# First modulation vectors with the raw weights stationary, and four weight pieces loaded ahead of the vectors' second half

## The chip, the cores and the metric

The kernel runs on one core of one Trainium2 chip. The metric is the device time of one execution in microseconds (us), from the first to the last instruction of the program with what lies around it; lower is better. The time before is 2695.26 us, the median of three runs (2690.73, 2696.66, 2695.26).

The core has five engines that run side by side and wait for each other through semaphores: TensorE (PE) for matrix products, VectorE (DVE), ScalarE (ACT), GpSimd (POOL), and SyncE (SP), which in this kernel issues nearly all transfers (DMAs). A matmul consists of a weight load (PEld in the profile), which puts the stationary operand into the array, and of the matmul proper, which moves the other operand past it, column by column.

## The reference

One layer of a backbone: a modulated RMSNorm, a mixer with one shared input projection, a gated residual, a second modulated norm and an MLP. There are 17 tiles of 128 tokens: tile 0 is context, tiles 1 to 16 are latent tokens. Context and latent tokens have a conditioning vector each (c_ctx and c), so all modulation vectors exist twice. What the change touches is this part:

```python
def modulation(cond, w_mod_l, b_mod_l):
    m = jax.nn.silu(cond) @ w_mod_l + b_mod_l
    return jnp.split(m[:, None, :], N_MOD, axis=-1)
...
    sh1, sc1, ga1, sh2, sc2, ga2 = mod
    h = rmsnorm(x, norm_mix_l) * (1.0 + sc1) + sh1
    o, s_new = mixer(h, s0, n_chunks, w_in_l, conv_l, a_log_l, dt_bias_l, o_norm_l, ws_l, bs_l, w_out_l)
...
    proj = h @ w_in_l
```

The model width is 1024, so each of the six modulation vectors has 1024 elements and w_mod is 1024 x 6144. The first norm needs sh1 (columns 0 to 1023 of w_mod) and sc1 (columns 1024 to 2047). Everything is float32.

## The kernel before

**Number formats.** The large products run three times on operands split into a high and a low part (mm3, lines 217 to 219: high x high, low x high or high x low). split_w (line 191 on ACT, line 192 on DVE) splits a weight piece of 128x512. The first modulation vectors are not split: mod_columns multiplies plain float32, for which TensorE runs each matmul as two records, each with a weight load of its own.

**Buffers.** Pieces of 128x512 come from one pool, tag "w", 49 buffers; raw_w (line 182) loads one of 256 KB. The tag "x" has three buffers of 128x1024. pm1() gives one of two PSUM banks, pt() one of three, pj() one of three.

**The start.** The conditioning vectors, through silu, stand in scond: for each of the 8 pieces k of the width, 128 rows by 2 columns (context, latent). mod_load(half, c0) loads eight pieces of w_mod, 512 columns of one vector: m0 is the first half of sh1, m1 that of sc1, m2 and m3 the second halves. mod_columns then needs the result as columns: feature on the partition, one column per conditioning vector. It does so in three steps. Eight matmuls with scond[:, k, :] stationary (128x2) move the raw piece (512 columns) and add up to a row pair of 2x512 in PSUM (line 321). ACT copies the pair to SBUF (line 323). Four transposes (line 326) turn its 128-column pieces into columns in a second PSUM bank. DVE adds the bias (line 329), and for sc1 adds 1 and multiplies by the norm's weight (line 333), into b1 and a1.

**The halo and the first tokens.** xh holds the ten token rows at the borders of the token blocks, in a buffer of the tag "x". norm_rows (ACT line 304, POOL line 176, DVE line 306) scales rows to unit size; eight transposes (line 373) bring xh into columns, hal. Then the three tiles of block 0 are loaded into buffers of the same tag "x" (line 378) and normalised; the third of them takes the buffer that xh had, and so waits for xh's transposes.

**Block 0.** first_half(half) modulates four pieces of hal (lines 393 to 397). column(k) of prep_block makes the modulated, transposed input of piece k: three transposes (line 468), ACT's scale and shift with a1 and b1 (line 470), and DVE's split into kH and kL (lines 473 and 474), which SP stores (lines 486 and 487). Step k of feature_tile (project) multiplies one 128x128 part of the weight piece W1[gi][k] with kH and kL: three matmuls of 388 columns. Three feature tiles run together in block 0, nine matmuls for each k. ab_block (lines 595 and 596) is a small projection of the same input. So steps k 0 to 3 need the first halves of sh1 and sc1 and the first four pieces of W1[1], steps k 4 to 7 the second halves and the other four.

**Order.** The text of the program doesn't set the order on an engine. A scheduler, which runs a simulated timeline while the program is built, takes what is ready, with the order of the text as a priority. In the text the loads of m2 and m3 come first, then those of four pieces of W1[1] (wr), then mod_columns(m1), steps k 0 to 3 of block 0, and mod_columns(m2) and (m3).

Of the kernel before, what the change touches and what calls it, by code (L numbers as in the profile page):

```python
# [8 lines left out]
F32 = mybir.dt.float32  # L9
# [8 lines left out]
P = 128  # L18
D = 1024
KT = D // P  # L20
# [41 lines left out]
def hybrid_step(  # L62
# [7 lines left out]
    V, A, G, T = nc.vector, nc.scalar, nc.gpsimd, nc.tensor  # L70
# [41 lines left out]
    ident = cp.tile([P, P], F32, name="ident")  # L112
# [49 lines left out]
    scond = cp.tile([P, KT, 2], F32, name="scond")  # L162
# [6 lines left out]
    def pm1():  # L169
        return pmp.tile([P, 512], F32, tag="pm", name="pm", bufs=2)  # L170
# [9 lines left out]
    def raw_w(src, pool=None, tag="w"):  # L180
        t = (pool or wp).tile([P, 512], F32, tag=tag, name="raw")
        load(out=t, in_=src)
        return t
# [83 lines left out]
    with ExitStack() as ph:  # L267
        p1 = ph.enter_context(tc.tile_pool(name="p1", bufs=2, reuse_waits="tile"))
        pf = ph.enter_context(tc.tile_pool(name="p1f", bufs=2, reuse_waits="tile"))
# [43 lines left out]
        def mod_load(half, c0):  # L313
            return [raw_w(w_mod[0, k * P : (k + 1) * P, c0 + half * 512 : c0 + half * 512 + 512])
                    for k in range(KT)]

        def mod_columns(raws, half, dst, bias, scaled):

            pm = pm1()
            for k in range(KT):  # L320
                T.matmul(pm[0:2, :], scond[:, k, :], raws[k], start=k == 0, stop=k == KT - 1)  # L321
            row = p1.tile([2, 512], F32, tag="mrow", name="mrow", bufs=1)
            A.copy(row, pm[0:2, :])
            pc = pm1()
            for i in range(4):
                T.transpose(pc[:, 2 * i : 2 * i + 2], row[:, i * P : (i + 1) * P], ident[0:2, 0:2])
            ks = slice(half * 4, half * 4 + 4)
            d = dst[:, :, ks]
            V.tensor_tensor(out=d, in0=pc[:, 0:8].rearrange("p (k c) -> p c k", c=2),
                            in1=bias[:, ks].unsqueeze(1).to_broadcast([P, 2, 4]), op=ALU.add)  # L330
            if scaled:
                for cd in range(2):
                    V.scalar_tensor_tensor(out=dst[:, cd, ks], in0=dst[:, cd, ks], scalar=1.0,
                                           in1=vec[:, 16 + half * 4 : 20 + half * 4], op0=ALU.add, op1=ALU.mult)
# [23 lines left out]
        convw = vec[:, 32:68].rearrange("p (w a) -> p w a", w=3)  # L358
        m1 = mod_load(0, D)
        mod_columns(m0, 0, b1, vec[:, 0:8], False)  # L360


        xh = p1.tile([P, D], F32, tag="x", name="xh", bufs=3)[0:10, :]
        for m in range(5):
            r0 = 255 + 384 * m
            load(out=xh[2 * m : 2 * m + 2, :], in_=x_sample[0, r0 : r0 + 2, :])
# [9 lines left out]
        for t in BLOCKS[0]:  # L376
            x = p1.tile([P, D], F32, tag="x", name="x", bufs=3)
# [5 lines left out]
        def load_w1(gi, ks):  # L383
            return [w1_raw(gi, k) for k in ks]

        def w1_raw(gi, k):
            return raw_w(w_in[0, k * P : (k + 1) * P, gi * 512 : (gi + 1) * 512])
# [327 lines left out]
        blk, xs_, cols = prep_block(0)  # L715
        for st in xs_:
            st()
        m2 = mod_load(1, 0)
        m3 = mod_load(1, D)
        wr = load_w1(1, range(4))  # L720
        mod_columns(m1, 0, a1, vec[:, 8:16], True)
        W1[1] += [split_w(r) for r in wr]
        first_half(0)
# [3 lines left out]
        wr = load_w1(0, range(KT))  # L727
        us = [feature_tile(blk, 0, 1, h) for h in range(3)]
        for k in range(4):
            cols[k]()  # L730
            for u in us:
                u["main"][k]()
        mod_columns(m2, 1, b1, vec[:, 0:8], False)
        mod_columns(m3, 1, a1, vec[:, 8:16], True)
        W1[1] += [split_w(r) for r in wk]
# [1016 lines left out]
    raws, sops = {}, {}  # L1752
# [91 lines left out]
    for m, (n, i, u, q) in enumerate(todo):  # L1844
# [20 lines left out]
        if i in (1, 5, 6) and mm < 28:  # L1865
            while pending and mm >= pending[0][0] + 2:
                _, k, r = pending.pop(0)
# [60 lines left out]
```

## Time and profile before

| | |
|---|---|
| median of three runs | 2695.26 us (2690.73 to 2696.66) |
| the profiled execution | 2696.7 us |
| its span, from first to last instruction | 2695.0 us |
| mean granted clock of TensorE | 0.993 |
| busy: TensorE, its weight loads, DVE, ACT, POOL | 2628.5, 2192.3, 1866.8, 1245.5, 229.5 us |
| the 64 records of line 321 | 30.5 us |

How to read it. Views quoted are of one profiled execution; times are us from the start of its span unless marked ns. L321 is line 321 of the kernel. In a group, "out<-in" names tiles, then come partitions x elements and the count, busy time and mean ns of one, and the idle time of the engine just before with what ended it. In the timeline and in the chain of waits, the first number is the start, the second the duration. Matmuls are pipelined: a row of several overlapping matmuls gives the time from the start of the first to the end of the last, so the pace is that time less one duration, over the count less one. In a table of windows stand the length, then busy us and count of PE, PEld, DVE, ACT and POOL, the granted clock of TensorE (1.00 is full), the mean busy share of the 16 DMA engines, and GB/s.

### The profile page before, as it was taken

To read this page: it belongs to the slowest core of one execution; us is meant where nothing else is said; L and a number is where in the kernel's file an instruction comes from. 1 tells how busy PE (TensorE), PEld (TensorE's weight loads), DVE (VectorE), ACT (ScalarE), POOL (GpSimd) and SP (SyncE) were. 2 spreads that over 40 slices of the span, in tenths; PEclk is the share of its full clock that TensorE was granted. 3 is DMA by queue.
4 is the path that set the end of the run, shared out by engine and by line. 5 is a ranking of instruction groups with operands and counts; after the bars stand their busy time and mean duration, and the time that the engine had idled before them with its cause. 6 is when DMAs were issued, how large, how long until landed. Compare 5 with 4: busy or idle time off the path is not lost.

```text
span 2695.0 us, 45202 instructions
## 1 busy us (share of the span) xinstructions
PE 2628.5 (98%) x15698; PEld 2192.3 (81%) x15698; DVE 1866.8 (69%) x3909; ACT 1245.5 (46%) x3092; POOL 229.5 (9%) x448
## 2 busy tenths in 40 slices
PE   8999999999999899999999999999999999999998
PEld 5999997788887787778887788888888787888887
DVE  5867656877777878885688775665565547774874
ACT  4655555555555656763355543332342432342441
POOL 3111203111111111110000000000000000000000
PEclk9999999999999999999999999999999999999999
DMA  8867539555555657885877797433459979876772
GB/s 297 279 202 224 183 113 299 177 157 161 160 162 157 204 191 232 269 279 181 285 221 228 212 313 228 122 104 106 121 170 371 329 265 309 272 243 215 235 252 94
DMA packets 569388, 580.91 MB, mean 216 GB/s; under 512 B 35693, under 2 KB 401693, under 8 KB 565575
## 3 DMA queue, kind: packets, MB, share of 16 engines
q1 hardware_dynamic: 569158, 578.03, 67.2%
q8 instruction: 123, 2.02, 0.3%
q14 instruction: 107, 0.87, 0.1%
HBM read 398.14 MB, written 179.74 MB: 214 GB/s over the span
## 4 chain that ended last, share of the span: by engine, by line
PE 86%; DVE 6%; DMA 5%; issue 1%; ACT 1%; POOL 0%; SPq 0%; DVEq 0%; POOLq 0%; ACTq 0%
PE f L219 17%; PE f L217 17%; PE f L218 17%; PE pj L217 6%; PE pj L219 6%; PE pj L218 6%; PE pd L959 3%; PE pm L217 1%; PE pm L219 1%; PE pm L218 1%; PE pm L321 1%; PE pt L575 1%; PE pd L1136 1%; PE pd L1137 1%; DMA qT<-qT_d 1%
## 5 line engine op out<-in xcount | busy, mean ns | idle before, releaser
L217 PE MATMUL f<-hop,zH 128*128 128x512 f32 x960 | 376.5, 393 | 1.2 <-ACT zH L1444 1.2
L218 PE MATMUL f<-hop,zH 128*128 128x512 f32 x960 | 377.1, 393 | 0.0
L219 PE MATMUL f<-hop,zL 128*128 128x512 f32 x960 | 376.9, 393 | 0.0
L217 PE MATMUL f<-hop,wH 128*128 128x512 f32 x896 | 354.0, 397 | 0.0
L219 PE MATMUL f<-hop,wL 128*128 128x512 f32 x896 | 351.3, 392 | 0.0
L218 PE MATMUL f<-hop,wH 128*128 128x512 f32 x896 | 351.1, 392 | 0.0
L1444 ACT CAST zH<-zraw 128x512 fp32r<-128x512 f32 x240 | 146.6, 620 | 287.2 <-DVE zraw L1438 86.4
L217 PEld LDWEIGHTS f<-hop,zH 128*128 128x128 f32 x960 | 180.3, 188 | 43.7 <-ACT zH L1444 1.6
L219 PEld LDWEIGHTS f<-hop,zL 128*128 128x128 f32 x960 | 180.3, 188 | 41.9 <-issue 0.9
L218 PEld LDWEIGHTS f<-hop,zH 128*128 128x128 f32 x960 | 180.2, 188 | 41.8 <-issue 0.9
L1438 DVE TENSOR_TENSOR zL<-zraw,zH 128x512 fp32r<-128x512 f32 x240 | 162.9, 686 | 69.1 <-ACT zH L1444 57.7
L219 PEld LDWEIGHTS f<-hop,wL 128*128 128x128 f32 x896 | 168.5, 188 | 37.7
L218 PEld LDWEIGHTS f<-hop,wH 128*128 128x128 f32 x896 | 168.8, 188 | 35.2
L217 PEld LDWEIGHTS f<-hop,wH 128*128 128x128 f32 x896 | 168.8, 188 | 34.7
L217 PE MATMUL pj<-kH,wH 128*128 128x386 f32 (+2 forms) x568 | 190.5, 338 | 0.3 <-DVE kH L473 0.3
L219 PE MATMUL pj<-kH,wL 128*128 128x386 f32 (+2 forms) x568 | 190.3, 335 | 0.0
L218 PE MATMUL pj<-kL,wH 128*128 128x386 f32 (+2 forms) x568 | 189.5, 334 | 0.0
L176 POOL TENSOR_TENSOR r<-rsq,nhalf 128x1 f32<-128x1 f32 (+1 forms) x38 | 23.0, 606 | 1499.3 <-DVE rsq L175 1499.3
L1438 DVE TENSOR_TENSOR wL<-raw,wH 128x512 fp32r<-128x512 f32 x112 | 76.0, 687 | 76.0 <-ACT wH L1444 74.9
L523 DVE SCALAR_TENSOR_TENSOR cv<-pj,vec,cv 128x384 f32<-128x384 f32 (+2 forms) x164 | 87.1, 539 | 58.7 <-ACT cv L520 57.4
L217 PEld LDWEIGHTS pj<-kH,wH 128*128 128x128 f32 x568 | 107.2, 189 | 4.6 <-issue 4.2
L217 PE MATMUL pj<-wH,hH 128*128 128x512 f32 x248 | 109.8, 443 | 0.0
(398 smaller groups left out, 6088.3 us busy)
## 6 DMA issues: line engine op xcount, KB each, us to landing
zraw<-z_d SPq DMA_DIRECT2D x212, 256.0 KB
raw<-in_w_ff_dram SPq DMA_DIRECT2D x128, 256.0 KB
hop<-hop_d SPq DMA_DIRECT2D x28, 1024.0 KB
z_d<-c SPq DMA_DIRECT2D x96, 256.0 KB
zraw<-s_d SPq DMA_DIRECT2D x96, 256.0 KB
raw<-in_w_mod_dram SPq DMA_DIRECT2D x80, 256.0 KB
r<-in_w_ff_dram SPq DMA_DIRECT2D x80, 256.0 KB
s_d<-s SPq DMA_DIRECT2D x64, 256.0 KB
```

Source lines behind the costliest of these rows:

```text
L176: G.tensor_tensor(out=out, in0=t[:np_, :n], in1=nhalf[:np_, :n], op=ALU.pow)
L217: T.matmul(ps, lh, rh, start=first and i == 0, stop=False, skip_group_check=more)
L218: T.matmul(ps, lh, rl, start=False, stop=False, skip_group_check=more)
L219: T.matmul(ps, ll, rh, start=False, stop=last and i == n - 1, skip_group_check=more)
L321: T.matmul(pm[0:2, :], scond[:, k, :], raws[k], start=k == 0, stop=k == KT - 1)
L523: V.scalar_tensor_tensor(out=cv[:, o : o + m], in0=ps[:, s + sh : s + sh + m], scalar=convw[:, w, j : j + 1], in1=cv[:, o : o + m], op0=AL ...
L575: T.matmul(ps[:, i * P : (i + 1) * P], kTt[:, i * P : (i + 1) * P], rhs[:, i * P : (i + 1) * P], start=True, stop=True)
L959: T.matmul(p[:, h, :], lhs[:, h, :], rhs[:, h, :], start=True, stop=True)
L1136: T.matmul(p[:, h, :], u["qT"][:, h, :], s[:, h, :], start=True, stop=False)
L1137: T.matmul(p[:, h, :], u["QK"][:, h, :], u["vn"][:, h, :], start=s is None, stop=True)
L1438: V.tensor_tensor(out=out, in0=a, in1=b, op=op)
L1444: A.copy(h, src)
```

## The change

mod_columns loses the row pair, its copy and its transposes. The raw weights become the stationary operand: for each k, four weight loads of 128x128 (times two records), each with a matmul that moves scond[:, k, :], two columns. All 32 matmuls add up in eight columns of one PSUM bank, of which the first starts the accumulation and the last ends it. xh gets a tile of its own, in another pool. The loads of four pieces of W1[1] move ahead of those of m2 and m3 in the text.

```diff
         def mod_columns(raws, half, dst, bias, scaled):
 
-            pm = pm1()
+            pc = pm1()
             for k in range(KT):
-                T.matmul(pm[0:2, :], scond[:, k, :], raws[k], start=k == 0, stop=k == KT - 1)
-            row = p1.tile([2, 512], F32, tag="mrow", name="mrow", bufs=1)
-            A.copy(row, pm[0:2, :])
-            pc = pm1()
-            for i in range(4):
-                T.transpose(pc[:, 2 * i : 2 * i + 2], row[:, i * P : (i + 1) * P], ident[0:2, 0:2])
+                for i in range(4):
+                    T.matmul(pc[:, 2 * i : 2 * i + 2], raws[k][:, i * P : (i + 1) * P], scond[:, k, :],
+                             start=k == 0 and i == 0, stop=k == KT - 1 and i == 3)
             ks = slice(half * 4, half * 4 + 4)
...
-        xh = p1.tile([P, D], F32, tag="x", name="xh", bufs=3)[0:10, :]
+        xh = pf.tile([P, D], F32, tag="xh", name="xh", bufs=1)[0:10, :]
...
         for st in xs_:
             st()
+        wr = load_w1(1, range(4))
         m2 = mod_load(1, 0)
         m3 = mod_load(1, D)
-        wr = load_w1(1, range(4))
         mod_columns(m1, 0, a1, vec[:, 8:16], True)
```

## The prediction

> **What bounds the kernel now.** I read the page first, then the chain of waits of the first 45 us, then the groups of instructions in that stretch, then single rows for the pace of weight loads, then windows with the granted clock.
>
> ```profile
> PE 86%; DVE 6%; DMA 5%; issue 1%; ACT 1%; POOL 0%; SPq 0%; DVEq 0%; POOLq 0%; ACTq 0%
> ```
>
> TensorE (PE) makes up 86% of the chain. So a microsecond of TensorE time saved or added at the start moves the end by about that much, unless a later wait takes it up.
>
> ```profile
> 1.23 3.20 DMA raw<-in_w_mod_dram
> 4.56 9.40 PE pm L321 x16
> ...
> 23.43 6.97 PE pm L321 x16
> ...
> 38.56 0.57 ACT mrow L323
> ...
> 40.57 0.59 PE pj L217 x2
> ...
> 44.78 0.18 PE pj L218
> ```
>
> These pieces (start, us, what) are the first load, the first and the third of the four calls of mod_columns (16 records each, since a float32 matmul is two), and what follows. TensorE does the calls one after another from 4.56 to 38.5, and the first matmul of the projection (L217) stands at 40.57, then one every 0.18 us. The order is not that of the program text: the second-half calls are written behind the projection's steps k 0 to 3, and ran ahead of them. The first call takes 9.40, the third 6.97: 2.4 us go to a slow clock at the start.
>
> ```profile
> L321 PE MATMUL pm<-raw,scond 128*2 128x512 f32 x64 | 30.5, 632 | 4.6 <-DMA raw<-in_w_mod_dram 4.6
> L326 PE MATMUL pm<-ident,mrow 2*128 2x2 f32 x16 | 1.6, 200 | 1.9 <-ACT mrow L323 1.9
> ```
>
> **The change, part by part.**
>
> *A. The matmuls turned round.* 64 records that move 512 columns past a stationary operand of 2 columns (30.5 us) become 8 x 4 x 2 records x 4 calls = 256, each with a weight load of 128x128 float32 and a matmul that moves 2 columns. The trace has no such pair. Its pace lies between these loads (PEld) of 128 columns:
>
> ```profile
> 21.97 0.57 PEld L373 LDWEIGHTS pt<-ident,xh 10*128 10x128 f32 x8 [0.86 <-DVE rsq L175]
> 427.88 0.53 PEld L654 LDWEIGHTS pt<-scr,mcum 128*128 128x128 f32 x4
> 929.05 1.81 PEld L959 LDWEIGHTS pd<-vn,kt 128*128 128x128 f32 x8
> ...
> L217 PEld LDWEIGHTS pj<-kH,wH 128*128 128x128 f32 x568 | 107.2, 189 | 4.6 <-issue 4.2
> L373 PEld LDWEIGHTS pt<-ident,xh 10*128 10x128 f32 x8 | 0.6, 136 | 0.9 <-DVE rsq L175 0.9
> 464.74 0.33 PEld L219 LDWEIGHTS pm<-wH,hL 128*128 128x128 f32 x1
> ```
>
> One load lasts 0.19 at full clock (the L217 group), so four in 0.53 follow each other at (0.53 - 0.19) / 3 = 0.11. L654's matmuls move 68 columns each; 0.11 is the pace of its loads, so fewer columns won't make it faster. L373, transposes, go at (0.57 - 0.14) / 7 = 0.06. L959 at 929.05 ran at half clock, as L219 at 464.74, where one load lasts 0.33, so (1.81 - 0.33) / 7 = 0.21. So: 0.06 as the lower bound, 0.11 at full clock, 0.21 at half clock. At full clock four calls cost 256 x 0.11 = 28.2, no gain to speak of against 30.5. The question is the clock.
>
> Pairs of windows of 3.41 us, half as long as the slow stretch from 927.53 to 934.35, show what keeps it (columns after the window: busy us of PE, PEld, DVE, ACT, POOL with counts, then the granted clock):
>
> ```profile
> 849.02:852.43 3.41, 1.79 (x11) 1.29 (x10) 2.61 (x7) 0.73 (x2) 1.61 (x3) 1.00 0.22 64
> 852.43:855.84 3.41, 2.55 (x31) 2.05 (x31) 3.34 (x8) 1.17 (x3) 0.30 (x1) 1.00 0.51 172
> 924.11:927.53 3.42, 1.83 (x20) 1.44 (x20) 3.42 (x14) 1.96 (x7) 0.90 (x3) 1.00 0.51 182
> 927.53:930.94 3.41, 2.96 (x24) 2.76 (x23) 3.41 (x16) 1.66 (x4) 1.70 (x3) 0.50 0.37 111
> 934.35:937.77 3.42, 3.42 (x42) 3.41 (x41) 3.27 (x10) 2.27 (x6) 0.00 (x0) 1.00 0.20 77
> ```
>
> ```profile
> 1108.43:1111.85 3.42, 1.47 (x13) 1.26 (x13) 3.42 (x10) 1.57 (x6) 1.46 (x2) 1.00 0.93 299
> 1111.85:1115.26 3.41, 3.41 (x9) 2.65 (x8) 3.31 (x11) 0.25 (x1) 1.62 (x2) 0.50 1.04 369
> ```
>
> After 849.02 to 852.43 the clock stayed at 1.00; after 924.11 to 927.53 it fell to 0.50 and was back at 1.00 from 934.35 on. The window that lost it had more records (20 against 11), and a little more busy time of matmuls and of loads. What it had less of is columns moved:
>
> ```profile
> L959 PE MATMUL pd<-vt,T 128*128 128x128 f32 x8 | 1.2, 288 | 0.0
> L1032 PE MATMUL pd<-Y,As 128*128 128x64 f16 x4 | 0.3, 191 | 0.3 <-ACT Y L1048 0.3
> L1047 PE MATMUL pd<-X,P 128*128 128x64 f16 x4 | 0.3, 193 | 0.0
> L1045 PE MATMUL pd<-P,X 128*128 128x64 f16 x4 | 0.3, 190 | 0.4 <-DVE P L1036 0.4
> ...
> L217 PE MATMUL pj<-wH,hH 128*128 128x512 f32 x2 | 0.9, 434 | 0.0
> L218 PE MATMUL pj<-wL,hH 128*128 128x512 f32 x2 | 0.8, 391 | 0.0
> L219 PE MATMUL pj<-wH,hL 128*128 128x512 f32 x2 | 0.8, 388 | 0.0
> ```
>
> 8 x 128 + 12 x 64 = 1792 columns lost it, 6 x 512 = 3072 and a few more kept it. (The window from 1108.43 lost it with little busy time, 1.47, so columns need not be all that counts.) The new stream moves 3.41 / 0.11 x 2 = 62 columns in such a window. I therefore take the clock as half in it. Before, the first call with its 512-column matmuls opened the clock itself.
>
> The Trainium skill (page "TensorE: Matmul & The Clock Gate", section "What's actually happening") lets the gate follow how busy the engine was in windows of about 3.4 us. Taken as "loads count too", that rule gives the second rival below; the windows at 849 and 924 speak against it, as loads did not hold the clock there.
>
> First two calls at half clock: 128 x 0.21 = 26.9. The second-half calls come beside or behind 36 projection matmuls of 388 columns, which open the clock; a stream that follows keeps it for a window or so. I take half of their 128 records at each pace: 64 x 0.11 + 64 x 0.21 = 20.5. A = 26.9 + 20.5 - 30.5 = **+16.9** (from +10.5, all 128 at 0.11, to +23.3, all at 0.21).
>
> *B. Row copy and transposes go.* The L326 group's 1.6 busy and 1.9 of waiting for the copy: **-3.5**. DVE's additions stay.
>
> *C. The projection restarts on a half clock.* One such start lost 9.40 - 6.97 = 2.4; it can happen behind the first two calls and behind the last: **+4.8** (2.4 to 4.8).
>
> *D. Four pieces ahead, halo rows in a tile of their own.* SP's queue, in order:
>
> ```profile
> 16.03 10.02 SPq L182 DMA_DIRECT2D raw<-in_w_mod_dram  x16
> 26.38 1.00 SPq L182 DMA_DIRECT2D raw<-in_w_in_dram  x2
> 27.81 0.33 SPq L378 DMA_DIRECT2D x<-in_x_sample_dram  x1
> 28.41 1.00 SPq L182 DMA_DIRECT2D raw<-in_w_in_dram  x2
> ```
>
> The four pieces (L182, w_in) and the third token tile (L378, which had to wait for the halo tile's buffer) stood behind 16 loads; now they pass them, some 10 us earlier, and the 16 land 5 x 0.63 = 3 us later. No byte is added. TensorE had other work in that time, so this only changes the order: steps k 0 to 3 can run before the second-half calls. Then those steps no longer hide the path from a finished call through DVE and ACT to the next kH: 38.56 to 40.57, 2.0 us, at two places. Pieces of the next call and the small ab projection cover part: **+1.5** (0 to 4).
>
> *E. Given back later.*
>
> ```profile
> 40.00:130.00 90.00, 87.76 (x523) 83.39 (x522) 74.05 (x181) 61.11 (x173) 20.64 (x57) 1.00 0.86 277
> ```
>
> From 40 to 130 TensorE idles 90.00 - 87.76 = 2.2 us; with TensorE later, loads and casts are ahead of it: **-1.5** (0 to -2.2).
>
> **Sum:** 16.9 - 3.5 + 4.8 + 1.5 - 1.5 = +18.2. The profiled execution took 2696.7 (span 2695.0 and 1.7 around it), 1.4 above the median of 2695.26; so 2696.7 + 18.2 - 1.4 = **2713.5**. With all low ends +7.2, 2702.5; with all high ends +28.6, 2723.9.
>
> **The rivals.**
>
> *1. The order doesn't change* (the order of each engine comes from a simulated timeline, which already ran against the text once). Then all four calls run in a row at half clock: 23.3 - 3.5 + 2.4 + 1.5 - 1.5 = +22.2, 2717.5. For it: L321 at 23.43 ahead of L217 at 40.57. Against it: the pieces and the token tile are now there first.
>
> *2. The clock opens all the same*, because loads count as work or short matmuls count for more than their columns: the other side. Decided by whether the 128x128 loads of L321 show 0.19 or 0.33 after 10 us. Then 28.2, and 23 records of the first 4.8 us at 0.10 more, are 30.5: A is 0, C is 0, B -3.5, D +1.5, E -0.5, together -2.5: 2692.8. For it: full-time load work, unlike any window above; 1792 and 3072 columns leave room for a part per matmul. Against: 20 loads didn't hold it where 10 did.
>
> *3. The pairs go at the transposes' 0.06.* 256 x 0.06 = 15.4, so loads set the end: last second-half load issued at 16.03 + 3 + 10.0 = 29, landed 3.2 later like the first load (1.23, 3.20), then 2.0: about 34.5 with k 0 to 3 done, against 40.57 + 36 x 0.18 = 47. About -12: 2683. Against it: L654. [...]
>
> **Chances and range.** Forecast 0.60, rival 1 0.08, rival 2 0.25, rival 3 0.07. About 0.2%, 5.4 us, can be told from no change. Slower: 0.60 + 0.08 + 0.02 of rival 2 = 0.70. Within: 0.20 of rival 2. Faster: 0.07 + 0.03 of rival 2 = 0.10. Range 2690 to 2722: it takes in most of rival 2 and leaves out rival 3 and the top of the forecast; the forecast's own range is 2702 to 2724.
>
> **What would show it.** The granted clock reads 0.50 after the first calls or L321's loads last 0.33: A right; 0.19 from 10 us on: rival 2. L326 gone and no idle before L321's second call: B. The first L217 matmuls twice 0.18 apart: C. L217 between the second and third call: D; behind all four: rival 1. Loads under 0.14: rival 3. If the two middle windows mislead about what the clock counts, the forecast falls whole.

## The result, and the profile after

| | before | after |
|---|---|---|
| median | 2694.32 us (2690.73 to 2696.66, six runs) | 2720.38 us (2711.77 to 2721.57, six runs) |
| the profiled execution | 2696.7 us | 2715.39 us |
| its span | 2695.0 us | 2713.6 us |

The changed kernel is slower by 0.9%: the ratio of the medians is 1.0093, with a 95% interval from 1.0080 to 1.0105. Between the two profiled executions the difference is 18.7 us, where +18.2 was forecast; between the medians it is 26 us. The profiled execution is one of the faster ones of the changed kernel, and why is a question for the experiments.

The groups of instructions of the first 90 us of the changed kernel, the new matmuls and their weight loads:

```profile
L322 PEld LDWEIGHTS pm<-scond,raw 128*128 128x128 f32 x256 | 48.0, 291 | 4.0 <-DVE abW L311 4.0
L322 PE MATMUL pm<-scond,raw 128*128 128x2 f32 x256 | 47.4, 320 | 4.0 <-DMA raw<-in_w_mod_dram 4.0
```

The 256 pairs take 47.4 us, to the tenth what the forecast had (26.9 + 20.5). Where they lie, and at what pace, shows in TensorE's timeline (start, us, engine, line, operation, count):

```profile
4.01 18.05 PE L322 MATMUL pm<-scond,raw 128*128 128x2 f32 x84 [4.01 <-DMA raw<-in_w_mod_dram]
22.95 9.55 PE L322 MATMUL pm<-scond,raw 128*128 128x2 f32 x44
33.03 5.54 PE L322 MATMUL pm<-scond,raw 128*128 128x2 f32 x26
38.44 0.99 PE L217 MATMUL pj<-kH,wH 128*128 128x388 f32 x2
39.23 0.53 PE L217 MATMUL pt<-kH,wH 128*128 128x388 f32 x1
...
42.77 3.09 PE L322 MATMUL pm<-scond,raw 128*128 128x2 f32 x26
...
48.70 0.53 PE L219 MATMUL pj<-kH,wL 128*128 128x388 f32 x1
...
55.52 9.49 PE L322 MATMUL pm<-scond,raw 128*128 128x2 f32 x64
...
67.79 0.53 PE L218 MATMUL pj<-kL,wH 128*128 128x388 f32 x1
...
70.37 0.34 PE L217 MATMUL pj<-kH,wH 128*128 128x388 f32 x1
```

The first 84 matmuls need (18.05 - 0.33) / 83 = 0.21 us each, the pace taken for half clock, and the next 44 the same. The projection's first matmuls, at 38.44 and 39.23, are at half clock too: one takes 0.53 where one at full clock takes 0.34, as at 70.37. The 26 matmuls at 42.77 go at 0.11: the clock is open there, behind the first projection matmuls. It shuts again behind these pairs: at 48.70 a projection matmul takes 0.53 (the granted clock is 0.50 from 46.5 to 49.9). Of the last call's 64, the mean is (9.49 - 0.33) / 63 = 0.15: it starts at full clock and ends at half. At 67.79 the projection restarts at 0.53 once more.

Windows of 4 us of the changed kernel (busy us and count of PE, PEld, DVE, ACT, POOL, then granted clock, DMA share, GB/s) show the clock shut. (Up to 43 us the column reads 1.00 because no change had been recorded yet; there only the pace tells.)

```profile
56.00:60.00 4.00, 4.00 (x38) 4.00 (x38) 0.00 (x0) 0.00 (x0) 0.00 (x0) 1.00 0.08 27
60.00:64.00 4.00, 4.00 (x21) 4.00 (x21) 0.00 (x0) 0.00 (x0) 0.00 (x0) 0.51 0.00 0
```

From 56 to 60 TensorE is busy 4.00 of 4.00 with nothing but pairs, and from 60 on, the same work runs on half the clock.

Where the rest went can be added up at one mark that both kernels have: the start of the 144th matmul of block 0's projection (72 for each three feature tiles), counted in TensorE's timeline, at 73.0 before and at 92.2 after, which is 19.2 later. The windows up to it, before:

```profile
0.00:4.56 4.56, 0.00 (x0) 0.03 (x1) 1.92 (x13) 1.50 (x2) 3.85 (x26) 1.00 0.48 139
4.56:40.57 36.01, 33.76 (x93) 7.90 (x94) 10.32 (x36) 11.09 (x20) 8.94 (x60) 1.00 1.01 354
40.57:73.00 32.43, 32.43 (x195) 31.81 (x196) 28.08 (x83) 22.42 (x54) 9.19 (x21) 1.00 0.79 260
```

and after:

```profile
0.00:4.01 4.01, 0.00 (x0) 0.03 (x1) 1.96 (x13) 1.50 (x2) 3.29 (x21) 1.00 0.41 125
4.01:38.44 34.43, 34.43 (x165) 34.38 (x166) 9.42 (x31) 8.39 (x15) 9.82 (x65) 1.00 0.96 342
38.44:92.20 53.76, 52.71 (x294) 51.30 (x295) 29.89 (x85) 25.10 (x55) 8.53 (x20) 0.87 0.65 208
```

TensorE's busy time went from 33.76 + 32.43 = 66.2 to 34.43 + 52.71 = 87.1, so +20.9. Of that the pairs are 47.4 - 30.5 = +16.9 and the transposes of L326 -1.6; the other +5.6 is the rest of the work at half clock, which is nearly the same up to the mark (203 records beside the 256, and 208 beside the 80 before). TensorE's idle time inside went from 2.25 to 53.76 - 52.71 = 1.05, and the first weights came 0.55 earlier. 20.9 - 1.2 - 0.55 = 19.2. From there on nothing comes back: the 1701st projection matmul starts at 429.6 before and 448.9 after, 19.3 later, and the span is 18.6 longer.

The waits of TensorE up to 93 us, after (us in total, times, longest), are two short ones beside that for the first weights (left out here):

```profile
PE pj L218 <- DVE kL L471: 0.6, 1, 0.6
PE pt L465 <- ACT full L467: 0.4, 1, 0.4
```

### The profile page after: what moved, and what is told of

It is laid out like the page before. It is cut to its first block, busy times and chain, and to the rows that moved or that the text cites. A ratio compares the mean times of both kernels' runs of the same rounds, so it can differ in the third digit from the quotient of the medians.

```text
span 2713.6 us, 45563 instructions
## 1 busy us (share of the span) xinstructions
PE 2649.3 (98%) x15874; PEld 2239.6 (83%) x15874; DVE 1866.1 (69%) x3909; ACT 1246.5 (46%) x3088; POOL 230.6 (8%) x448
## 4 chain that ended last, share of the span: by engine, by line
PE 83%; DMA 7%; DVE 6%; ACT 2%; issue 2%; SPq 0%; POOL 0%; DVEq 0%; POOLq 0%; ACTq 0%
PE f L219 16%; PE f L217 16%; PE f L218 16%; PE pj L217 6%; PE pj L219 6%; PE pj L218 6%; PE pd L956 2%; PE pm L322 2%; DMA qT<-qT_d 2%; PE pm L217 1%; PE pm L219 1%; PE pm L218 1%; PE pt L572 1%; DMA hop_d<-opH 1%; PE pt L532 1%
## 5 line engine op out<-in xcount | busy, mean ns | idle before, releaser
L217 PE MATMUL f<-hop,zH 128*128 128x512 f32 x960 | 376.5, 393 | 1.2 <-ACT zH L1441 1.2
L217 PE MATMUL f<-hop,wH 128*128 128x512 f32 x896 | 354.4, 397 | 0.0
L217 PEld LDWEIGHTS f<-hop,zH 128*128 128x128 f32 x960 | 180.4, 188 | 43.7 <-ACT zH L1441 1.6
L217 PEld LDWEIGHTS f<-hop,wH 128*128 128x128 f32 x896 | 169.0, 189 | 34.8
L217 PE MATMUL pj<-kH,wH 128*128 128x386 f32 (+2 forms) x568 | 192.3, 341 | 0.8 <-DVE ab L604 0.6
L520 DVE SCALAR_TENSOR_TENSOR cv<-pj,vec,cv 128x384 f32<-128x384 f32 (+2 forms) x164 | 87.3, 541 | 61.6 <-ACT cv L517 60.3
L217 PEld LDWEIGHTS pj<-kH,wH 128*128 128x128 f32 x568 | 108.1, 191 | 5.5 <-issue 3.6
L217 PE MATMUL pj<-wH,hH 128*128 128x512 f32 x248 | 110.4, 445 | 0.0
```

Of the source, the lines that this page charges most:

```text
L217: T.matmul(ps, lh, rh, start=first and i == 0, stop=False, skip_group_check=more)
L520: V.scalar_tensor_tensor(out=cv[:, o : o + m], in0=ps[:, s + sh : s + sh + m], scalar=convw[:, w, j : j + 1], in1=cv[:, o : o + m], op0=AL ...
```

## The experiments

**Which part of the change costs.** Four kernels take it apart. The first has the columns turned round in the kernel before, without the new order and halo tile:

```diff
-                T.matmul(pm[0:2, :], scond[:, k, :], raws[k], start=k == 0, stop=k == KT - 1)
...
+                for i in range(4):
+                    T.matmul(pc[:, 2 * i : 2 * i + 2], raws[k][:, i * P : (i + 1) * P], scond[:, k, :],
+                             start=k == 0 and i == 0, stop=k == KT - 1 and i == 3)
```

> The kernel before with the new mod_columns alone; load order and halo tile as before. Theory: all four calls run in a row at half clock, 256 x 0.21 = 54 us on 30.5 before, less 3.5 for copies and transposes, plus 2.4 for one slow restart of the projection: 2712 to 2722 us. Rival (turned-round matmuls are cheap, the order costs): 2690 to 2698 us.

Measured: 2721.01 us (2717.97 to 2727.34), ratio 1.010 (1.008 to 1.012). The expected time came, but not quite the expected way: three of the four calls run ahead of the projection, which starts at 47.7, the fourth between its steps with the clock open for most of its pairs, and the 256 pairs take 50.6 us, not 54. The new columns alone cost what the whole change costs.

The second is the changed kernel with mod_columns as before, so with the new order and the halo tile only:

```diff
+                T.matmul(pm[0:2, :], scond[:, k, :], raws[k], start=k == 0, stop=k == KT - 1)
+            row = p1.tile([2, 512], F32, tag="mrow", name="mrow", bufs=1)
...
-                    T.matmul(pc[:, 2 * i : 2 * i + 2], raws[k][:, i * P : (i + 1) * P], scond[:, k, :],
```

> The changed kernel with the old mod_columns (row pair, copy, transposes); the four pieces ahead and the halo rows' own tile stay. Theory: the new order by itself moves the time little, 2690 to 2698 us, with the clock at 1.00 throughout the first 100 us. Rival (the order costs most of the 26 us, by uncovered waits): over 2705 us.

Measured: 2709.94 us (2707.10 to 2716.78), ratio 1.0059 (1.0041 to 1.0077). The expectation fell: the order by itself costs some 13.5 us (against 2696.45 of the kernel before, beside it). TensorE's timeline and the windows of this kernel:

```profile
25.62 3.56 PE L321 MATMUL pm<-raw,scond 128*2 128x512 f32 x4 [0.18 <-DMA raw<-in_w_mod_dram]
29.11 0.62 PE L217 MATMUL pj<-kH,wH 128*128 128x388 f32 x2
...
43.88 7.03 PE L321 MATMUL pm<-raw,scond 128*2 128x512 f32 x16
```

```profile
20.00:24.00 4.00, 2.78 (x15) 1.04 (x13) 1.72 (x4) 2.70 (x5) 1.37 (x3) 1.00 1.00 340
24.00:28.00 4.00, 3.09 (x8) 0.78 (x9) 3.62 (x16) 2.43 (x6) 1.30 (x5) 0.71 1.05 402
52.00:56.00 4.00, 3.74 (x22) 3.03 (x21) 3.93 (x15) 1.66 (x5) 1.10 (x4) 1.00 0.36 101
56.00:60.00 4.00, 2.32 (x13) 1.60 (x12) 4.00 (x19) 3.49 (x8) 3.20 (x6) 0.98 0.40 128
```

The projection starts at 29.11, 11.5 us earlier than before, and yet its 144th matmul starts at 80.4 instead of 73.0. TensorE idles 2.1 us from 20 to 28, waiting for normalised tokens and the copied row, and 1.9 us from 52 to 60, behind the last call: the path from a finished call to kH, which steps k 0 to 3 no longer hide, as they have been done. Each idle stretch is followed by a loss of clock, from 25.7 to 29.1 (25.62: four records of 512 columns in 3.56, where at full clock 16 take 7.03) and from 59.8 to 63.2. A later wait of 2.8 us, projection matmuls behind VectorE's convolution, and a third loss of clock come after 110 us. In the changed kernel the same order shows 1.0 us of waits: its pairs at half clock give the other engines the time. The costs of the two parts don't add up: alone they are 24.6 (2721.01 - 2696.45) and 13.5 us, together 26 us.

The halo tile alone and the four pieces alone, each in the kernel before:

```diff
-        xh = p1.tile([P, D], F32, tag="x", name="xh", bufs=3)[0:10, :]
+        xh = pf.tile([P, D], F32, tag="xh", name="xh", bufs=1)[0:10, :]
```

> The kernel before with the halo rows' own tile alone. Theory (the order costs where the projection's first steps run ahead of the second-half calls and leave two waits uncovered; that needs weight pieces that are there early): the second-half calls still run first, 2691 to 2699 us. Rival (the early third token tile alone moves the steps): 2703 to 2712 us as in the run with the old mod_columns.

```diff
+        wr = load_w1(1, range(4))
         m2 = mod_load(1, 0)
         m3 = mod_load(1, D)
-        wr = load_w1(1, range(4))
```

> The kernel before with the four pieces loaded ahead alone; the third token tile still waits for the halo rows' buffer. Theory: steps k 0 to 3 still wait for that tile, the order of TensorE keeps the second-half calls first, 2691 to 2699 us. Rival (the pieces' loads delay the second-half pieces and that costs by itself): 2700 to 2712 us.

Measured: 2694.61 us, ratio 0.9998 (0.9987 to 1.0009), for the tile; 2699.40 us, ratio 1.0013 (1.0003 to 1.0024), for the pieces, against 2696.51 before. The second lies 0.4 us above its range, a loss of 0.13% that is barely clear of none. In both, all four calls still run ahead of the projection, which starts at 38.79 and 41.64. So neither alone makes the new order; in these kernels with the row pair, only with the third token tile and the weight pieces both early did the scheduler put steps of the projection between the calls.

**What the clock follows.** In the next four, each matmul moves more columns: scond's two columns repeated, the extra results in PSUM unread. The weight loads and their number stay. In the changed kernel:

```diff
-                    T.matmul(pc[:, 2 * i : 2 * i + 2], raws[k][:, i * P : (i + 1) * P], scond[:, k, :],
+                    T.matmul(pc[:, 128 * i : 128 * i + 128], raws[k][:, i * P : (i + 1) * P],
+                             scond[:, k, :].unsqueeze(1).to_broadcast([P, 64, 2]),
...
```

> The changed kernel, but each matmul of the first vectors moves 128 columns (the two conditioning columns 64 times over, by a repeated read) past the same 128x128 weight load; the loads stay 256, only two of each 128 result columns are used. Theory (the clock is held by columns moved, the loads' own pace is 0.11 us at full clock): the granted clock opens by about 13 us and stays open, loads last 0.19, the 256 pairs take 29 to 33 us instead of 47.4, and the run comes to 2693 to 2700 us. Rival (loads of raw weights are slow by themselves, or the new order is what costs): pairs still near 47 us or the time still 2712 to 2722.

With 32 and with 64 columns in place of 128:

> As the run with 128 columns, but 32 columns per matmul (a quarter). Theory with columns alone: at half clock a pair of 0.21 us streams for a quarter of its time, below the windows that kept the clock, so it stays at half and the time at 2712 to 2722 us. Rival (each matmul counts for more than its columns): the clock opens and the time is that of 128 columns, 2693 to 2700 us.

> As the run with 128 columns, but 64 columns per matmul. Theory (the clock counts the time in which columns stream): 64 columns fill about half of a pair's 0.21 us at half clock, more than the window that kept the clock with 6 x 512 columns, so the clock opens before 15 us and the time is that of 128 columns, 2700 to 2708 us. Rival (it takes nearly full streaming): half clock as with 2 and 32 columns, 2715 to 2725 us.

And 128 columns in the kernel before, without the new order and halo tile:

> The kernel before with mod_columns turned round and 128 columns moved per matmul; loads and halo tile as before. Theory: with the clock held and the second-half calls in their old place, the pairs take some 31 us as the row matmuls did and the copies and transposes (3.5 us) are saved: 2690 to 2695 us, the fastest of all. Rival (turning round costs by itself, or the saved waits come back elsewhere): 2696 to 2705 us.

Measured: 2702.62 us (ratio 1.0032, 1.0018 to 1.0047) with 128 columns, 2711.29 (1.0064, 1.0041 to 1.0086) with 64, 2721.75 (1.0101, 1.0086 to 1.0116) with 32, and 2703.97 (1.0031, 1.0018 to 1.0043) with 128 in the old order. Only the run with 32 columns came within the range that its theory gave; 128 columns in the new order took 2.6 us more than that, 64 lie between theory and rival, and 128 in the old order lie in the rival's range. The first row of pairs in TensorE's timeline, with 32 columns, with 64, and with 128:

```profile
4.32 18.10 PE L322 MATMUL pm<-scond,raw 128*128 128x32 f32 x84 [4.32 <-DMA raw<-in_w_mod_dram]
```

```profile
4.39 18.15 PE L322 MATMUL pm<-scond,raw 128*128 128x64 f32 x84 [4.39 <-DMA raw<-in_w_mod_dram]
```

```profile
4.43 15.97 PE L322 MATMUL pm<-scond,raw 128*128 128x128 f32 x124 [4.43 <-DMA raw<-in_w_mod_dram]
```

With 2, 32 and 64 columns, 84 pairs fill the same 18.1 us: half clock for the whole stretch. With 128, 124 pairs fit into 15.97 us. All 256 take 33.6 us there (29 to 33 were expected), against 47.4:

```profile
L322 PE MATMUL pm<-scond,raw 128*128 128x128 f32 x256 | 33.6, 293 | 4.4 <-DMA raw<-in_w_mod_dram 4.4
```

More work per matmul made the stream faster: what had kept the clock shut was how little the matmuls move. The expectation for 64 columns, an open clock before 15 us, fell: by the 7.03 / 16 = 0.44 us of 512 columns, 64 take 0.055 at full clock, an estimate, half of the 0.11 between two loads, and being in use for half of the time did not open it. Once open, behind the first projection matmuls, it stayed open with 64 columns through the last call, which with 32 columns and with 2 it did not:

```profile
52.00:60.00 8.00, 8.00 (x66) 8.00 (x64) 2.57 (x8) 0.00 (x0) 0.00 (x0) 1.00 0.24 78
```

```profile
52.00:60.00 8.00, 8.00 (x34) 8.00 (x32) 2.58 (x8) 0.00 (x0) 0.00 (x0) 0.51 0.28 91
```

(64 columns above, 32 below: 66 records against 34 in the same busy 8 us.)

Neither kernel with 128 columns beats the one before. In the new order the waits come out that the slow pairs had hidden, 3.3 us for normalised tokens and 2.1 for the halo's kH, and the clock, which was expected to stay open, shut once more: behind the first of them it reads 0.50 from 26 to 28 us. The two waits:

```profile
PE pt L466 <- DVE x L306: 3.3, 2, 1.9
PE pj L217 <- POOL kH L461: 2.1, 1, 2.1
```

In the old order, where 2690 to 2695 us and the fastest of all was expected, the pairs end at 37.1 (29.80 + 7.31) and the projection still starts at 40.66, as before at 40.57. TensorE's timeline there, then ScalarE's:

```profile
29.80 7.31 PE L322 MATMUL pm<-scond,raw 128*128 128x128 f32 x64
...
39.57 0.47 PE L343 MATMUL pm<-wH,abW 128*128 128x512 f32 x1 [2.35 <-ACT full L468]
...
40.66 0.59 PE L217 MATMUL pj<-kH,wH 128*128 128x388 f32 x2
```

```profile
33.42 1.06 ACT L304 ACTIVATE junk<-x 128x1024 bf16<-128x1024 f32 x1 [10.73 <-DMA x<-in_x_sample_dram]
...
35.78 2.58 ACT L191 CAST wH<-raw 128x512 fp32r<-128x512 f32 x4 [1.21 <-DMA raw<-in_w_in_dram]
...
39.09 0.91 ACT L468 ACTIVATE full<-pt,b,a 128x128 f32<-128x128 f32 x2
```

What bounds the start there is the third token tile, for which ScalarE waits until 33.4, and the weights that it casts ahead of the first kH, not the calls. So at full clock the new columns had nothing to win at this place. Its 144th projection matmul is at 74.5, 1.5 behind the kernel before, and its 1701st 1.9 behind; the rest of its 7.5 us comes later, and which order of work costs them was not taken apart.

**Opening the clock before the first call.** The 2.4 us that the first call lost to a shut clock were there to be won in the kernel before. Two matmuls of ones, whose result is not used, fill the time before the first weights land:

```diff
+        hot = pt()
+        T.matmul(hot, ones, ones.unsqueeze(1).to_broadcast([P, 4, P]), start=True, stop=True)
+        T.matmul(hot[:, 0:384], ones, ones.unsqueeze(1).to_broadcast([P, 3, P]), start=True, stop=True)
```

> The kernel before with two float32 matmuls of ones (512 and 384 columns) into an unused PSUM tile while the first weights are on their way; nothing reads them. Theory (the clock opens with columns moved): the clock opens one window of 3.4 us earlier, at 4.6 to 6 us in place of 9.3, the first call takes 7.0 to 8.0 us in place of 9.4, and the run comes 1 to 2.4 us lower, 2692 to 2696 us. Rival (a later wait takes it up or the reordered rest costs more): 2696 to 2702 us.

Measured: 2692.92 us (the median of twelve executions, of which one took 9170.23 us and the others 2691.20 to 2702.07), ratio 0.9998 without that one (0.9987 to 1.0009), no change. The time lies in the expected range, but so does that of the kernel before beside it, 2694.59. TensorE's timeline:

```profile
4.50 7.49 PE L324 MATMUL pm<-raw,scond 128*2 128x512 f32 x16
...
23.03 0.48 PE L471 MATMUL pt<-ident,x 128*128 128x128 f32 x1 [1.15 <-DVE x L309]
...
23.95 9.70 PE L324 MATMUL pm<-raw,scond 128*2 128x512 f32 x16
```

The first call fell from 9.38 to 7.49. But TensorE now came to the token transposes ahead of the third call sooner than the tokens did, and waited; the clock shut (0.50 from 24 to 28 us), and the third call took 9.70 where it took 7.03. What was won was lost within 30 us. The 144th projection matmul stands at 75.9, 2.9 later than before, and even that doesn't show in the medians.

**Why the medians are further apart than the profiles.** The changed kernel was profiled twice more, unaltered.

> The changed kernel again, for a second profile. Theory (the clock gate's windows run free of the program, so the half-clock stretches fall differently in each execution): the 256 pairs take between 45 and 52 us and the 144th projection matmul stands between 91 and 99 us, and the difference in span to the first profile stands there already. Rival (executions differ in a later stage): pairs and that matmul within 1 us of the first profile (47.4 and 92.2), the span different all the same.

> The changed kernel once more, with the same expectations: theory, pairs 45 to 52 us, the 144th projection matmul at 91 to 99 us, the difference in span there already; rival, both within 1 us of the first profile and the span different all the same.

Measured: 2722.66 and 2722.12 us. Their pairs take 49.5 and 50.0 us, and their 144th projection matmuls stand at 98.9 and 96.8, 6.7 and 4.6 later than in the first profile, of 7.3 and 6.8 us that they are behind at the end. So the theory held nearly in full for the one; in the other some 2 us came later in the kernel. Between the 72nd and the 144th projection matmul they lose 4.7 and 4.4 us on the first profile. ScalarE's timeline in the first of them:

```profile
83.14 1.06 ACT L418 ACTIVATE junk<-x 128x1024 bf16<-128x1024 f32 x1 [4.04 <-DMA x<-in_x_sample_dram]
...
84.45 1.06 ACT L418 ACTIVATE junk<-x 128x1024 bf16<-128x1024 f32 x1 [0.16 <-DMA x<-in_x_sample_dram]
...
85.50 1.33 ACT L517 ACTIVATE cv<-pj,vec 128x128 f32<-128x128 f32 x4
```

and TensorE's:

```profile
88.18 0.66 PE L217 MATMUL pj<-kH,wH 128*128 128x388 f32 x1 [2.93 <-DVE cv L520]
88.64 0.53 PE L218 MATMUL pj<-kL,wH 128*128 128x388 f32 x1
```

On ScalarE the square of the next block's tokens (L418) stands ahead of block 0's convolution (L517, then VectorE's L520), and waits for tiles that landed late; the convolution starts at 85.50, when the squares are done, and frees the PSUM buffer that TensorE's next feature tile needs. TensorE idles 2.93 us and then runs about ten matmuls at half clock (0.53 at 88.64). In the first profile the same instructions stand in the same order, and the tiles came earlier:

```profile
78.73 1.06 ACT L418 ACTIVATE junk<-x 128x1024 bf16<-128x1024 f32 x1 [0.94 <-DMA x<-in_x_sample_dram]
...
79.78 1.34 ACT L517 ACTIVATE cv<-pj,vec 128x128 f32<-128x128 f32 x4
```

So it hangs on when the tiles land: the convolution starts at 79.78 in the first profile, at 85.50 and 83.38 in the other two. To test it, the token tiles were given a fourth buffer, with the halo rows back among them, so that the next block's tiles are loaded long before:

```diff
-        xh = pf.tile([P, D], F32, tag="xh", name="xh", bufs=1)[0:10, :]
+        xh = p1.tile([P, D], F32, tag="x", name="xh", bufs=4)[0:10, :]
...
-                x = p1.tile([P, D], F32, tag="x", name="x", bufs=3)
+                x = p1.tile([P, D], F32, tag="x", name="x", bufs=4)
```

> The changed kernel with the halo rows back in the tag of the token tiles, which gets a fourth buffer (the same space as the halo's own tile), so that the next block's token tiles are loaded before ScalarE reaches them. Theory: the profiled execution of the changed kernel, 18.7 us above before, escaped a wait that most of its executions have. In two further profiles ScalarE waits at the square of the next block's tokens (L418) for a tile that landed at 83 to 84 us, the convolution of block 0 stands behind it, and TensorE idles about 2.8 us at 84 to 88 and restarts on half clock; their 144th projection matmul is 4.6 and 6.7 us behind that of the first profile. With the tiles early that wait goes: no idle of TensorE from 80 to 90, the 144th projection matmul at 91 to 94, and a median 3 to 6 us under the changed kernel's, 2714 to 2718; the pairs still take 47 to 50. Rival: the difference between the profiles is a drift over the whole kernel, and the median stays at 2719 to 2723.

Measured: 2718.76 us (2714.49 to 2720.00), ratio 1.0092 (1.0075 to 1.0109), a little above the 2714 to 2718 expected. The wait on the token tile is gone, and another has its place. ScalarE's timeline:

```profile
80.28 0.62 ACT L191 CAST wH<-raw 128x512 fp32r<-128x512 f32 x1 [3.93 <-DMA raw<-in_w_in_dram]
80.81 1.35 ACT L517 ACTIVATE cv<-pj,vec 128x128 f32<-128x128 f32 x4
```

Now the cast of a weight piece stands ahead of the convolution and waits 3.93 us for its transfer; TensorE idles 2.24 us at 81.9, and the 144th projection matmul is at 95.3, not at 91 to 94. The time is not distinguishable from the changed kernel's, so the expected gain of 3 to 6 us didn't come. What holds is the place, ScalarE's convolution behind something that waits for a transfer; that the tokens alone were the cause does not hold. How much of the 7 us between the profile and the medians it makes up is shown for two executions only.

No version beat the kernel before by more than a measurement can tell.

## Why the prediction was right, step by step

**The direction and the size were right by the forecast's own mechanism.** Rival 2, that the clock opens all the same, is out: the pairs of 2 columns ran at 0.21. Rival 1, all four calls in a row, is out too: in the changed kernel L217 stands at 38.44, inside the third call, of which 38 pairs follow it. The kernel with the new columns alone comes nearest to that rival, with three calls ahead. Rival 3 is out: the best pace of a longer stretch of pairs was 0.11.

**A, +16.9.** Measured +16.9 in the profiled execution, +19 to +19.5 in the two later ones. The first two calls ran at half clock throughout, as foreseen. Of the later 128 pairs, counted by their start against the granted clock, 52 ran at half clock in the profiled execution, 74 and 77 in the two later ones, where the forecast took 64. So the mechanism held, and the agreement to the tenth is luck: 25 pairs more at 0.10 us each are the 2.5 us between the executions.

The Trainium skill (page "TensorE: Matmul & The Clock Gate", section "What's actually happening") lets the clock follow how busy the engine was in a window of about 3.4 us. This case agrees only if busy is not read as the profile's busy time: PE and PEld were both busy 4.00 of 4.00 from 56 to 60, and the clock shut at 60. The forecast's reading, columns moved, stood the test at 2, 32, 64 and 128 columns; whether the columns count, or the time in which they stream, these runs don't tell apart. The Trainium skill (same page, section "Back-to-back issue gap") says that in a stream of pairs of a weight load and a matmul both set the spacing. This case agrees that the matmul's columns alone don't: with a new 128x128 float32 load each, 2, 64 and 128 columns went at 0.11 us at full clock, and nothing went faster.

**B, -3.5.** The transposes' 1.6 us and their 1.9 us of waiting are gone; the waits after name neither.

**C, +4.8.** Measured +5.6: the two restarts that were foreseen, at 38.4 and behind the last call, where the projection goes on at 67.5, and a third that was not, from 46.5 to 49.9, where the clock had shut again behind the 26 pairs at 42.77. With the projection some transposes and the small projection's matmuls ran at half clock too.

**D, +1.5 (0 to 4).** 1.0 us of waits appeared, within the bounds, but the reason given for a small term was wrong, so this is luck. With the old columns the order costs 13.5 us, of which 7.4 by the 144th projection matmul. The forecast had the path of 2.0 us at two places; it didn't have that each such gap also shut the clock there, nor the waits after 110 us. In the changed kernel the slow pairs covered this. The price hangs on the columns: with 128 columns the new order and the old come to the same ratio (1.0032 and 1.0031), and with 2 columns to 1.0093 and 1.010. A forecast that had rightly seen the clock stay open (rival 2, 2692.8) would still have been some 10 us low: the kernel with 128 columns took 2702.62, of which the pairs' 33.6 in place of 30.5 explain 3.

**E, -1.5.** Not given back: 19.2 at the 144th matmul, 19.3 at the 1701st, 18.6 at the end. Only the earlier first weights, 0.55, and 0.3 of small waits went the forecast's way.

**The scale.** This is the step that was off: the forecast went from the profiled execution to the median by -1.4, and the changed kernel's median is 5.0 above its profiled execution, in part for a wait that comes in some executions and not in others, and for pairs that run at half clock in greater number. The sum was right for the execution that was profiled, and that this was one of the faster is luck; against the median it is 7 too low, which itself lies near the upper edge of the range.

## What to carry to other kernels

A matrix-vector product with the matrix stationary kept TensorE busy all the time here, and yet its clock at half. Where the stationary operand changes with every matmul, count the columns moved: 64 a load, by estimate half of the time between two loads, did not open the clock here, and 128 did. Time a reordering with the other part of a change undone before believing that it is free, since the slow pairs hid most of the waits behind them. And where an engine holds a buffer's release, as ScalarE's convolution did here, look at what stands ahead of it in that engine's order: taking one late transfer out of the way brought up the next.

## What the runs showed of the hardware that was not expected

A stream of 128x128 float32 loads is paced by the clock like the matmuls: 0.21 us a pair at half clock and 0.11 at full clock, alike for 2, 32 and 64 columns. Opening and holding differ: 64 columns a load did not open the clock through the first two calls, and held it through the last call of 64 pairs once it was open; 32 columns did neither (the clock shut at 52.2, in the last call).
